# Matmul with batch norm on one core: one more block turned raw, late copies of x by VectorE and ScalarE instead of GpSimd, and one block turned by transfer instead of by TensorE

## The chip, the core and the metric

The kernel runs on one core of a Trainium2 chip. TensorE (PE in the profile, its weight loads PEld), VectorE (DVE), ScalarE (ACT), GpSimd (POOL) and SyncE (SP, which here only issues transfers) each work through a queue of their own, in order, and wait for each other by semaphores. The metric is the device time of one execution in microseconds; less is better.

## The reference

```
y = np.matmul(x, weight)                        # (16, 512, 1024) x (1024, 768), float32
mean = np.mean(y, axis=(0, 1), keepdims=True)   # one mean per output column
var = np.var(y, axis=(0, 1), keepdims=True)
y_norm = (y - mean) / np.sqrt(var + eps)
return (gamma * y_norm + beta).astype(np.float32)
```

The 16 x 512 rows of x are taken as 8192 rows. Each of the 768 columns needs its mean and variance over all 8192 rows before any element of it can be stored. x is 32 MB, the output 24 MB.

## The kernel before, in words

x is loaded in 16 chunks of 512 rows, cast to bf16 on the way (L402, issued by POOL), and turned by DVE (L431, L424) so that the sum dimension k lies on the partitions. The 768 columns are six column tiles of 128 (`nt` 0 to 5). Tiles 0 and 1 (`GA` = 2) are computed with rows on the partitions while x streams in (L506). Tiles 2 to 5 are computed with the columns on the partitions: the weights stand still, a chunk of x moves, and eight matmuls of 128x512 (L571) make one chunk of one tile in one PSUM bank. For chunks 0 to 3 (`EARLY`) this happens while x is still arriving; for chunks 4 to 15 it happens tile after tile once x is complete: tile 2, 3, 4, 5. Tile 3 takes the chunks in the order 12 to 15, 4 to 11, tile 4 in the order 4 to 11, 12 to 15.

After each chunk VectorE takes the statistics from PSUM (L707) and ScalarE keeps y in bf16 in SBUF (L711). When a tile's 16 chunks are done, `finish_tasks` aggregates the statistics (L972, VectorE), takes the root (L986, ScalarE) and makes scale and shift (L989 to L993, VectorE). Then the tile goes out in eight blocks of two chunks (`col_block`). A block has to be normalized and turned, because it lies column by row and the output is row by column. There are three ways:

- *xact*: VectorE (ScalarE for tile 2) normalizes y in place (L1022), SP issues a transfer that turns it (L1214), ScalarE converts it to float32 (L1226), SP stores it (L1196).
- *pe*: VectorE normalizes (L1022), TensorE turns eight 128x128 pieces into a PSUM bank (L1040; the planner puts each between two matmuls of a column unit), ScalarE copies it out of PSUM (L1204), SP stores it (L1196). `MODE` says which blocks of a tile use which way; before, all blocks of tile 4 are *pe*.
- *raw* (`RAW`, `raw_turn`, `raw_spread`, `raw_block`): y is turned by transfer before its statistics are known (L1102, right after the last load of x, because chunks 0 to 3 are ready by then). Once they are known, scale and shift are turned from columns into rows: VectorE prepares them (L1135, L1136), four copies gather them into one row (L1139, 32x64), three copies deal the row to all partitions (L1139, 32x256), and ScalarE puts it into a PSUM bank (L1152). Gather and deal can each go to POOL or to ScalarE. Then VectorE multiplies the turned block from that bank (L1168), POOL adds the shift (L1172), SP stores (L1176). Before, blocks 0 and 1 of tiles 2 and 4 are raw.

The last block of tile 4 is held back and stored in the tail (L1246, L1249). Tile 5 is the tail: after its last matmul come the last statistics, the root (L1302), scale and shift (L1315), and then block by block norm (L1339), turn (L1040), copy (L1352) and store (L1355).

For most chunks x is turned so that pairs of k stand side by side. `part_chunk` copies such a chunk into two plain halves (`x_pl`, L543), four copies of 128x1024 a chunk, so that later matmuls read it without a stride. Chunks 4, 5, 7, 8, 9 and 10 (`PARTED`) are copied early, by ScalarE. Chunks 12 to 15 (`LATE`) are copied after tile 3 has read them, for tiles 4 and 5; the engine is chosen by the planner from those listed.

The order of the work is made by a list planner (`arrange`): every piece of work is a task with a due time, an engine or a choice of engines with a guessed duration, and slots in pools (eight PSUM banks, SBUF tiles, a ring of SBUF words). It places the tasks in a simulated order, and the program then issues them in that order on each engine. All stores and transposing transfers share SP's queue in that order.

The numbering of lines is that of the kernel before; in the changed kernel lines after L1116 stand two to five lines further down.

Of the kernel before, what the change touches and what calls it, by code (L numbers as in the profile page):

```python
# [227 lines left out]
def kernel(  # L228
# [19 lines left out]
    P = 128  # L248
# [14 lines left out]
    EARLY = 4  # L263
# [3 lines left out]
    GY = 2  # L267
# [4 lines left out]
    XT, YB, SQ = C - EARLY, 28, 3  # L272
    ADDED = (0,6,16,28,40)
    PARTED, LATE, SINGLE = (4,5,7,8,9,10), (12,13,14,15), (2,3,6)
    MODE = {2:'xact',3:'xact',4:('pe',)*8}
    MODE = {nt: m if isinstance(m, tuple) else (m,) * (C // GY) for nt, m in MODE.items()}
    RAW, RAWADD, RAWDUE = {2:(0,2),4:(0,2)}, {2:'POOL',3:'POOL',4:'POOL'}, {2:14.0,3:8.0,4:8.0}
    RING = 3 * CH // 32 * KQ // 2
    ENG = {"ACT": nc.scalar, "DVE": nc.vector, "POOL": nc.gpsimd, "SP": nc.sync}

# [39 lines left out]
    sum2 = singles.tile([P, 2 * NA], f32)  # L320
    sum3 = singles.tile([P, 2 * NA], f32)
# [33 lines left out]
    def task(prio, engines, emit, deps=(), lock=False, **kw):  # L355
        t = Task(prio, engines, emit, deps, **kw)
        t.lock = lock
        tasks.append(t)
        return t
# [14 lines left out]
    STORE, XBAR = 1 / 350.0, 1.25  # L374
# [63 lines left out]
    at = M - CH  # L438
# [5 lines left out]
    for kind, n, *n1 in order:  # L444
# [12 lines left out]
        if m0 == M // 2:  # L457
# [6 lines left out]
            dma=(rows * K * 4 / 1024 + 384 * also) * PER_KB * 1.024, takes=[slot])  # L464
# [4 lines left out]
        for i in range(rows // QR):  # L469
            c, q = divmod(m0 // QR + i, QPC)  # L470
# [9 lines left out]
        if rows % QR:  # L480
            t0 = rows // QR * QR // 32
            m1 = m0 + 32 * t0
            c, q = divmod(m1 // QR, QPC)
# [40 lines left out]
    def part_chunk(c, now, engines, small=False, step=0.0, after=()):  # L524

        src = x_slot[c]
        slots = [Slot(sqs if jw < SQ else ys) for jw in range(JW)] if small else [Slot(xts)] * JW
        ts = []

        def copy(jw):  # L530
            def emit(eng):
                if small:
                    if jw < SQ:
                        x_pl = sqpool.tile([P, 2, CH], bf16, tag="sq")
                    else:
                        x_pl = ypool.tile([P, 2, CH], bf16, tag="y")
                    slots[jw].tile = [x_pl]
                elif jw == 0:
                    x_pl = xtpool.tile([P, JW, 2, CH], bf16, tag="xT")
                    slots[0].tile = [x_pl[:, i] for i in range(JW)]  # L540
                dst = slots[jw].tile[0 if small else jw]
                pairs = src.tile[:, jw].rearrange("p m e -> p e m")
                seq(nc.scalar.copy(dst, pairs) if eng == "ACT" else ENG[eng].tensor_copy(dst, pairs))  # L543
            return emit

        for jw in range(JW):
            new = small or jw == 0
            ts.append(task(
                now + step * jw, engines, copy(jw), [x_ready[c, q, JW] for q in range(QPC)] + list(after) + ([] if new else ts[:1]),
                len(engines) > 1, uses=[src] + ([] if new else [slots[jw]]), takes=[slots[jw]] if new else []))  # L550
        plain[c] = slots, ts, small
# [41 lines left out]
    clock = [12.0]  # L593
# [29 lines left out]
    def col_unit(nt, c, jws, q0=0, q1=QPC):  # L623
        slot = bank_of.setdefault((nt, c), None) or Slot(banks)
        bank_of[nt, c] = slot
        first = jws[0] == 0 and q0 == 0
        xs = [plain[c][0][jw] for jw in jws] if c in plain else [x_slot[c]]
        kw = {"takes": [slot], "uses": xs} if first else {"uses": [slot] + xs}
        t = pe_task((1.728 if c in plain or c in SINGLE else 1.808) * len(jws) / JW * (q1 - q0) / QPC,
                    mm(nt, c, list(jws), slot, q0, q1),  # L630
                    waits(jws, c, q0, q1) + ([plain[c][1][jw] for jw in jws] if c in plain else []), (nt, c), **kw)
        if q1 - q0 == QPC:
            t.hosts = 4
        if jws[-1] == JW - 1 and q1 == QPC:
            col_stats(nt, c, slot, t)
        return t
# [60 lines left out]
    col_end = {}  # L697
# [148 lines left out]
    U = clock[0] - 30.0  # L846
# [66 lines left out]
    U = S - 30.0  # L913
# [38 lines left out]
    k = 0  # L952
# [139 lines left out]
    for c in range(RC, C):  # L1092
        ga_block(c, S - 29.8 + 35.5 * (c - RC))

    def raw_turn(nt, c):

        yslot, slot = y_of(nt, c), Slot(ys)

        def xbar(eng):
            r_sb = ypool.tile([P, GY * RT, P], bf16, tag="y")  # L1100
            slot.r = r_sb
            bi = nc.sync.dma_start_transpose(slot.r, y(nt, c, GY))  # L1102
            if not gated:
                tc.add_manual_dep(
                    bi.ins, gate.ins.name,
                    mybir.DependencyInfo(mybir.DependencyClass.Sync, mybir.DependencyReason.DATA),
                    reason="behind the loads",
                )
                gated.append(bi)
            seq(bi)  # L1110

        b = task(U, {"SP": (1.4, 1.4)}, xbar, [col_end[nt, c + i][1] for i in range(GY)] + [gate], dma=XBAR,
                 takes=[slot], uses=[yslot])
        raw[nt, c] = slot, b

    raw, gated, raw_aff = {}, [], {}  # L1116
    gate = last_loads[-1]
    for nt in RAW:
        for c in RAW[nt]:
            raw_turn(nt, c)  # L1120

    def raw_spread(nt, fin_task):
        bank = Slot(banks)
        k = sorted(RAW).index(nt)
        row = sum2[:, 2 * P * k:2 * P * (k + 1)].rearrange("p (i n) -> p i n", n=P)
        wide, turned = sum1[:, NA + 64 * k:NA + 64 * (k + 1)], sum3[:, 64 * k:64 * (k + 1)]
        both = turned.rearrange("p (i n) -> p i n", n=32)
        now = clock[0] + RAWDUE[nt] + 2.0

        def quadrant(i):  # L1130
            return slice(32 * i, 32 * i + 32)

        def turn(eng):
            for i, src in enumerate((scale, shift)):
                seq(nc.vector.tensor_copy(wide[:, quadrant(i)], src[:, nt:nt + 1].to_broadcast([P, 32])))  # L1135
            seq(nc.vector.transpose(turned, wide))  # L1136

        def move(eng, dst, src):
            seq(nc.scalar.copy(dst, src) if eng == "ACT" else nc.gpsimd.tensor_copy(dst, src))  # L1139

        def gather(eng):
            for i in range(4):
                move(eng, row[0:32, :, quadrant(i)], both[quadrant(i)])

        def deal(eng):
            for i in range(1, 4):
                move(eng, row[quadrant(i)], row[0:32])

        def keep(eng):
            a_ps = psum.tile([P, CH], f32, tag="b")  # L1150
            bank.tile = a_ps
            seq(nc.scalar.copy(a_ps[:, 0:2 * P], row.rearrange("p i n -> p (i n)")))  # L1152

        d = task(now, dve(0.35), turn, [fin_task], True)
        g = task(now, {"POOL": (0.8, 0.85), "ACT": (0.9, 1.0)}, gather, [d])
        s = task(now, {"POOL": (1.2, 1.25), "ACT": (1.0, 1.1)}, deal, [g])
        t = task(now, act(0.4), keep, [s], takes=[bank])
        raw_aff[nt] = bank, t, s, row[:, 1]
# [26 lines left out]
    def col_block(nt, c, due, fin_task, held=False):  # L1185
# [12 lines left out]
        a = task(due, act(1.144) if nt == GA else dve(0.45), norm(nt, c, GY), [fin_task] + keeps, nt > GA, uses=[yslot])  # L1198
        if MODE[nt][c // GY] == "pe":
            b, bank = turn_block(due + 0.5, nt, m0, count, [a], [yslot])  # L1200
# [11 lines left out]
        def xbar(eng):  # L1212
# [3 lines left out]
        b = task(due + 0.5, {"SP": (1.4, 1.4)}, xbar, [a], dma=XBAR,  # L1216
                 takes=[t_slot] + ([slot] if MODE[nt][c // GY] == "xact" else []), uses=[yslot])
        if MODE[nt][c // GY] == "xpool":
            def store_x(eng):
# [42 lines left out]
    for nt in range(GA, NT - 1):  # L1262
        if nt == NT - 2:
            for i, c in enumerate(LATE):
                part_chunk(c, clock[0] + 0.0 + 4.0 * i, {"POOL": (1.1, 1.15), "DVE": (0.63, 0.7)},
                           i == 0, 4.0 / 4, [col_end[NT - 3, late[-1]][1]])
        for c in CHUNKS[nt]:
            for jws in halves if nt > GA or c > EARLY + 2 else [[jw] for jw in range(JW)]:
                col_unit(nt, c, jws)
        f = finish_tasks(nt)  # L1270
        start = clock[0] + 3.0
        if nt in RAW:
            raw_spread(nt, f)
        for i in range(C // GY):
            if (nt, GY * i) in raw:
                raw_block(nt, GY * i, start + STEP[nt] * i + RAWDUE[nt])
                continue
            if nt == NT - 2 and C // GY - HELD <= i:
                held.append((nt, GY * i, f))
                continue  # L1280
            col_block(nt, GY * i, start + STEP[nt] * i, f)


    nt = NT - 1
# [45 lines left out]
    for c, r0, rows in ends:  # L1330
        due = E + 2.0 + 0.6 * c
        n = max(rows // CH, 1)
# [13 lines left out]
        b, bank = turn_block(due + 0.6 * (n - 1), nt, m0, count, norms, [y_of(nt, c + i) for i in range(n)])  # L1346
# [56 lines left out]
```

## Time and profile before

| what | value |
|---|---|
| median of three runs | 206.69 us (206.57 to 206.7) |
| the profiled execution, its time | 206.43 us |
| the profiled execution, its span | 204.6 us |
| busy: PE, DVE, ACT, POOL | 188.8, 158.5, 140.3, 129.5 us |
| DMA traffic | 48.48 MB, mean 237 GB/s |
| L1040 turns on PE | 112 |
| L543 late copies | 12 on POOL, 4 on DVE |
| transposing transfers | 14 of L1214, 4 of L1102 |

The profile is of one execution. The span runs from its first to its last instruction; the execution's own time is 1.8 us longer. A group's line gives line, engine, operation, tiles and shapes, the count, busy time and the mean of one in ns, and then the idle time ahead of these instructions with what ended it. The chain is followed back from the last instruction to what released it at each step. Matmuls are pipelined, so the record of one is longer than the distance to the next.

### The profile page before, as it was taken

What the parts mean: (1) busy time and instruction counts of PE and PEld (TensorE: products, weight loads), DVE (VectorE), ACT (ScalarE), POOL (GpSimd) and SP (SyncE); (2) the same over time, 40 slices, a digit from 0 to 9 for tenths busy, and PEclk for the clock granted to TensorE, in tenths of its full rate; (3) what the DMA queues carried; (4) which work ended last, traced back from release to release, by engine and by line L of the source; (5) the groups of instructions that cost most, each with busy time, mean ns of one, the idle gap of its engine ahead of it and who ended that gap; (6) DMA issues with size and microseconds to landing.
All of it is one profiled execution on the core that took longest, in us unless ns stands there. A gap on an engine that the chain in (4) does not pass through costs nothing.

```text
span 204.6 us, 3497 instructions
## 1 busy us (share of the span) xinstructions
PE 188.8 (92%) x1203; PEld 115.1 (56%) x1218; DVE 158.5 (77%) x243; ACT 140.3 (69%) x253; POOL 129.5 (63%) x153
## 2 busy tenths in 40 slices
PE   7979999999999999999999999999999999997900
PEld 3457554656488888777875444444444445554600
DVE  4031879999999999969989998978799879737900
ACT  2001461369979999998979766997555868975950
POOL 7776954877499989996404999389978402530000
PEclk9999999999999999999999999999999999999995
DMA  4999999999999999999594898999999999999998
GB/s 76 155 203 195 194 196 196 196 197 196 190 193 197 197 196 197 196 197 195 100 157 165 313 339 314 265 306 329 305 287 215 325 325 318 307 343 298 311 346 246
DMA packets 97522, 48.48 MB, mean 237 GB/s; under 512 B 23264, under 2 KB 96992, under 8 KB 97504
## 3 DMA queue, kind: packets, MB, share of 16 engines
q0 software_dynamic: 34624, 18.36, 65.0%
q1 hardware_dynamic: 62880, 29.90, 52.8%
q8 instruction: 9, 0.15, 0.3%
q14 instruction: 9, 0.07, 0.1%
HBM read 36.71 MB, written 25.17 MB: 302 GB/s over the span
## 4 chain that ended last, share of the span: by engine, by line
PE 79%; DMA 9%; ACT 3%; POOL 2%; issue 1%; DVE 1%; ACTq 0%; DVEq 0%; POOLq 0%
PE y_ps L571 50%; PE y_ps L506 21%; DMA w_sb<-in_weight_dram 6%; PE y_ps L810 4%; ACT o_sb L1352 3%; DMA ring<-in_x_dram 3%; PE o_ps L1040 2%; POOL ring L402 1%; PE y_ps L749 1%; POOL w_sb L386 1%; DVE xT_sb L431 1%; PE a_ps L899 1%; PE o_ps L1070 0%; ACTq L1398 0%; PE tot_ps L867 0%
## 5 line engine op out<-in xcount | busy, mean ns | idle before, releaser
L571 PEld LDWEIGHTS <-w_sb 128*128 128x128 bf16 x520 | 50.3, 97 | 57.6
L571 PE MATMUL y_ps<-xT_sb,w_sb 128*128 128x512 bf16 (+1 forms) x264 | 58.7, 371 | 0.4
L571 PE MATMUL y_ps<-x_pl,w_sb 128*128 128x512 bf16 x241 | 56.7, 379 | 0.4
L402 POOL DMA_DIRECT2D ring<-in_x_dram x76 | 47.3, 628 | 13.8 <-DVE xT_sb L424 5.0
L506 PE MATMUL y_ps<-w_sb,xT_sb 128*128 128x256 bf16 x448 | 50.5, 273 | 1.8 <-DMA ring<-in_x_dram 1.4
L506 PEld LDWEIGHTS <-xT_sb 128*128 128x128 bf16 x448 | 43.6, 98 | 9.4 <-DVE xT_sb L431 2.7
L431 DVE STREAM_TRANSPOSE xT_sb<-ring 128x1024 f32<-128x1024 f32 (+1 forms) x29 | 31.2, 1111 | 13.6 <-DMA ring<-in_x_dram 13.5
L711 ACT CAST y_sb<-y_ps 128x512 bf16<-128x512 f32 x51 | 29.1, 590 | 15.0 <-DVE stats L707 11.3
L707 DVE BATCH_NORM_STATS2 stats<-y_ps 128x6 f32<-128x512 f32 x46 | 30.8, 686 | 10.1 <-PE y_ps L571 9.8
L938 POOL TENSOR_TENSOR ring<-ring,sum 128x1024 f32<-128x1024 f32 (+1 forms) x11 | 23.7, 2182 | 15.0 <-DVE ring L933 14.9
L655 ACT ACTIVATE sq_sb<-y_ps 128x512 f32<-128x512 f32 x28 | 16.5, 613 | 17.1 <-PE y_ps L506 16.4
L662 POOL TENSOR_TENSOR sum<-sum,sq_sb 128x512 f32<-128x512 f32 x20 | 25.6, 1278 | 3.5 <-ACT sq_sb L655 2.3
L543 ACT COPY x_pl<-xT_sb 128x1024 bf16<-128x1024 bf16 x24 | 24.4, 1054 | 1.7 <-DVE xT_sb L431 1.7
L658 DVE TENSOR_TENSOR sum<-y_ps,sum 128x512 f32<-128x512 f32 x28 | 18.9, 675 | 6.4 <-ACT sq_sb L655 5.4
L668 ACT CAST y_sb<-y_ps 128x512 bf16<-128x512 f32 x28 | 16.0, 602 | 7.6 <-DVE sum L658 7.4
L933 DVE TENSOR_TENSOR ring<-y_sb,a_ps 128x1024 f32<-128x1024 bf16 (+1 forms) x16 | 16.7, 1077 | 0.1
L1040 PE MATMUL o_ps<-ident,y_sb 128*128 128x128 bf16 x112 | 14.8, 220 | 1.6 <-DVE y_sb L1339 1.5
L1226 ACT CAST ring<-ring 128x1024 f32<-128x1024 bf16 x14 | 14.7, 1049 | 1.8 <-DMA ring<-y_sb 1.8
L543 POOL COPY x_pl<-xT_sb 128x1024 bf16<-128x1024 bf16 x12 | 13.3, 1139 | 2.1 <-DVE x_pl L543 2.0
L424 DVE STREAM_TRANSPOSE xT_sb<-ring 128x2048 bf16<-128x2048 bf16 x6 | 13.5, 2288 | 0.2 <-DMA ring<-in_x_dram 0.2
L1139 POOL COPY sum<-sum 32x256 f32<-32x256 f32 (+1 forms) x10 | 3.4, 344 | 12.4 <-ACT sum L1139 11.6
L587 PE MATMUL idle_ps<-idle_sb 128*128 128x512 f32 x18 | 9.6, 685 | 1.5 <-DVE idle_sb L315 1.5
(105 smaller groups left out, 163.4 us busy)
## 6 DMA issues: line engine op xcount, KB each, us to landing
out_dram<-ring SPq DMA_DIRECT2D x37, 512.0 KB, 3.7
ring<-in_x_dram POOLq DMA_DIRECT2D x52, 256.0 KB, 8.7
out_dram<-o_sb SPq DMA_DIRECT2D x6, 512.0 KB, 4.8
ring<-in_x_dram POOLq DMA_DIRECT2D x16, 128.0 KB, 6.1
w_sb<-in_weight_dram POOLq DMA_DIRECT2D x8, 192.0 KB, 6.1
out_dram<-ring SPq DMA_DIRECT2D x6, 256.0 KB, 3.0
ring<-in_x_dram POOLq DMA_DIRECT2D x4, 192.0 KB, 7.8
out_dram<-o_sb SPq DMA_DIRECT2D x3, 256.0 KB, 2.6
```

The source lines that it names most:

```text
L402: bi = seq(nc.gpsimd.dma_start(x_bf[32 * i:32 * i + 32], src[:, :, KQ * i:KQ * (i + 1)]))
L431: seq(nc.vector.transpose(dst, src[:, :, jw0:jw1]))
L506: seq(nc.tensor.matmul(y_ps[:, s], x_of(c, jw, e, t * P, (t + 1) * P), w_sb[:, jw, e, 0:NA], start=(s == 0 and jw == 0 and e == 0), stop=( ...
L543: seq(nc.scalar.copy(dst, pairs) if eng == "ACT" else ENG[eng].tensor_copy(dst, pairs))
L571: seq(nc.tensor.matmul(y_ps, w_sb[:, jw, e, nt * P:(nt + 1) * P], moving(c, jw, e, q0 * QR, q1 * QR, parted), start=(jw == 0 and e == 0 an ...
L658: seq(nc.vector.tensor_add(sum1, slot.tile[:, 0:n], sum1))
L662: seq(ENG[eng].tensor_add(acc, acc, state["sq"][:, 0:n]))
L707: seq(nc.vector.bn_stats(dst, slot.tile))
L711: seq(nc.scalar.copy(y(nt, c), slot.tile))
L933: seq(nc.vector.tensor_mul(slot.o, y_row[c].y[:, s0:s1], aff[0][:, None, :].to_broadcast([P, n, NA])))
L938: seq(ENG[eng].tensor_add(slot.o, slot.o, row[:, None, :].to_broadcast([P, n, NA])))
L1040: seq(nc.tensor.transpose(dst, src, ident))
```

## The change

Three things are changed together.

1. `RAW` gets block 0 of tile 3. Its transfer is issued with the four other early ones, and tile 3 gets a spread of its own (a third row of scale and shift, placed in `sum3`), one VectorE multiply, one POOL add and one store, in place of norm, transfer, convert and store.
2. Block 2 of tile 4 (chunks 4 and 5) goes the way *xact* instead of *pe*.
3. The late copies of chunks 12 to 15 are offered to VectorE and ScalarE instead of POOL and VectorE.

`raw_turn` also takes a due time and could turn later blocks; no block of this change uses that.

```diff
-    MODE = {2:'xact',3:'xact',4:('pe',)*8}
+    MODE = {2:'xact',3:'xact',4:('pe',)*2+('xact',)*1+('pe',)*5}
     MODE = {nt: m if isinstance(m, tuple) else (m,) * (C // GY) for nt, m in MODE.items()}
-    RAW, RAWADD, RAWDUE = {2:(0,2),4:(0,2)}, {2:'POOL',3:'POOL',4:'POOL'}, {2:14.0,3:8.0,4:8.0}
+    RAW, RAWADD, RAWDUE = {2:(0,2),3:(0,),4:(0,2)}, {2:'POOL',3:'POOL',4:'POOL'}, {2:14.0,3:8.0,4:8.0}
...
-    def raw_turn(nt, c):
+    def raw_turn(nt, c, due):
...
-        b = task(U, {"SP": (1.4, 1.4)}, xbar, [col_end[nt, c + i][1] for i in range(GY)] + [gate], dma=XBAR,
+        b = task(due, {"SP": (1.4, 1.4)}, xbar, [col_end[nt, c + i][1] for i in range(GY)] + [gate], dma=XBAR,
                  takes=[slot], uses=[yslot])
...
     for nt in RAW:
         for c in RAW[nt]:
-            raw_turn(nt, c)
+            if c < EARLY:
+                raw_turn(nt, c, U)
...
         k = sorted(RAW).index(nt)
-        row = sum2[:, 2 * P * k:2 * P * (k + 1)].rearrange("p (i n) -> p i n", n=P)
+        acc, at = ((sum2, 0), (sum2, 2 * P), (sum3, 2 * P))[k]
+        row = acc[:, at:at + 2 * P].rearrange("p (i n) -> p i n", n=P)
...
             for i, c in enumerate(LATE):
-                part_chunk(c, clock[0] + 0.0 + 4.0 * i, {"POOL": (1.1, 1.15), "DVE": (0.63, 0.7)},
+                part_chunk(c, clock[0] + 0.0 + 4.0 * i, {"DVE": (0.63, 0.7), "ACT": (1.05, 1.1)},
                            i == 0, 4.0 / 4, [col_end[NT - 3, late[-1]][1]])
...
+        for c in RAW.get(nt, ()):
+            if c >= EARLY:
+                raw_turn(nt, c, clock[0])
```

In the order in which the changed program's instructions then stand, seven late copies are on ScalarE and nine on VectorE; POOL's queue after the adds of tiles 0 and 1 holds only the spreads and the raw adds; the gather of tile 4's spread is on POOL and its deal on ScalarE (before: the other way round); TensorE's turns of tile 4 stand beside chunks 7 to 10 of tile 5 (before: 8 to 12); and chunk 15 of tile 4 is computed in one piece (before: in two halves, between halves of chunks 4 and 5 of tile 5).

## The prediction

> **What bounds the kernel now.** I read the page's busy shares and chain first, then the chain in order of time, then a table by stage, then the groups by line, last the engines' timelines.
>
> ```profile
> PE 188.8 (92%) x1203; PEld 115.1 (56%) x1218; DVE 158.5 (77%) x243; ACT 140.3 (69%) x253; POOL 129.5 (63%) x153
> ...
> PE 79%; DMA 9%; ACT 3%; POOL 2%; issue 1%; DVE 1%; ACTq 0%; DVEq 0%; POOLq 0%
> ```
>
> TensorE carries 79% of the chain. In order of time (start, length, what) the chain stays on PE from 25.95 to 187.29 us:
>
> ```profile
> 171.06 0.06 PE o_ps L1040
> 171.12 0.22 PE y_ps L571
> 171.33 0.06 PE o_ps L1040
> ...
> 187.05 0.24 PE o_ps L1040 x4
> ...
> 187.94 0.20 ACT std L1302
> ...
> 190.04 4.74 ACT o_sb L1352 x6
> ```
>
> The reader is to see two things: a turn on PE (L1040) takes 0.06 us out of the chain between two matmuls, and after PE's last column unit comes a tail: root, norms, copies and stores of tile 5. By stage (length; PE, PEld, DVE, ACT, POOL busy; clock; DMA share; GB/s):
>
> ```profile
> 143.00:150.00 7.00, 6.95 (x33) 3.21 (x33) 5.50 (x10) 3.15 (x6) 6.94 (x7) 1.00 1.14 313
> 150.00:158.00 8.00, 7.94 (x38) 3.56 (x37) 8.00 (x13) 5.66 (x8) 5.99 (x6) 1.00 1.12 228
> 158.00:170.40 12.40, 12.35 (x58) 5.59 (x58) 9.79 (x20) 9.12 (x13) 2.98 (x3) 1.00 1.20 325
> ...
> 178.00:188.20 10.20, 9.45 (x67) 5.55 (x66) 5.11 (x13) 7.00 (x13) 2.84 (x2) 1.00 1.14 342
> 188.20:189.30 1.10, 0.27 (x3) 0.13 (x4) 1.03 (x5) 0.68 (x2) 0.00 (x0) 1.00 0.50 149
> 189.30:191.50 2.20, 2.16 (x27) 1.45 (x26) 2.20 (x8) 2.11 (x5) 0.00 (x0) 1.00 0.96 289
> ```
>
> PE is full wherever the change acts, at full granted clock. VectorE is full in 150-158; ScalarE has room; the stores have spare time in 150-158 and at 188-191. So only what shortens PE's own work, or makes PE wait, moves the end.
>
> **The change part by part.** Groups by line (busy, mean ns of one; idle before):
>
> ```profile
> L543 ACT COPY x_pl<-xT_sb 128x1024 bf16<-128x1024 bf16 x24 | 24.4, 1054 | 1.7 <-DVE xT_sb L431 1.7
> L1040 PE MATMUL o_ps<-ident,y_sb 128*128 128x128 bf16 x112 | 14.8, 220 | 1.6 <-DVE y_sb L1339 1.5
> L1226 ACT CAST ring<-ring 128x1024 f32<-128x1024 bf16 x14 | 14.7, 1049 | 1.8 <-DMA ring<-y_sb 1.8
> L543 POOL COPY x_pl<-xT_sb 128x1024 bf16<-128x1024 bf16 x12 | 13.3, 1139 | 2.1 <-DVE x_pl L543 2.0
> L1172 POOL TENSOR_TENSOR ring<-ring,sum 128x1024 f32<-128x1024 f32 x4 | 9.5, 2387 | 2.1 <-issue 2.1
> L543 DVE COPY x_pl<-xT_sb 128x1024 bf16<-128x1024 bf16 x4 | 3.1, 796 | 0.0
> ```
>
> *Block 2 of tile 4 by transfer.* Eight L1040 turns leave PE. While turns are interleaved the matmul starts go 171.22, 171.50, 171.77: 0.2717 us a pair, against 0.2159 us for a plain matmul (32 in 6.91 us from 134.26). So one turn is 0.056 us and eight are **0.45 us off the path**. The turns stop one chunk earlier; the other blocks' turns are the same. ScalarE reads the transfer's result (1049 ns) instead of PSUM (1015 ns, L1204): the same work. One DMA transpose is added at about 169-170.
>
> Here a rule speaks for far more. The row says 220 ns for one turn but they start 0.056 us after the matmul before. The Trainium skill, "TensorE: Matmul & The Clock Gate", Part 4, puts a turn in one kernel's context at about 275 ns; an estimate by that is 8 x 0.275 = 2.2 us. By the trace's starts it is 0.45 us, and the sum goes by these.
>
> *Block 0 of tile 3 raw.* Its transpose moves from about 150 to the head of SP's queue, behind the four others (6.34 us for four, 1.6 each, ending at 106.2). SP then waits 2.9 us for L1060 before the first store at 109.08, so 1.6 us hides there. Tile 3 loses one y norm (655 ns) and one L1226 on ScalarE, and gains L1135/L1136 (0.6-0.8 us) and one L1168 (1214 ns) on DVE, 2.2 us of gather and deal plus one L1172 (2387 ns) on POOL, and one L1152 (388 ns) on ACT that holds a PSUM bank for some 4 us. All off PE. In tile 4's own spread the gather goes to POOL and the deal to ACT: three 32x256 copies there, which the trace does not show. Bounds: 243 ns (ACT, 32x64) and 421 ns (POOL, 32x256); nearest 388 ns (ACT, 128x256), so 1.2 us.
>
> *Late copies.* POOL loses 12 copies (13.3 us). In the built order ACT gets 7 (7 x 1.054 = 7.4 us), DVE 5 more (9 in all; 5 x 0.796 = 4.0 us). ACT idles 3.85 us in 143-150, 2.34 in 150-158, 1.0 in 140-143: 7.2 us against 7.4 + 0.4 - 1.0 = 6.7. Just enough. DVE has only 1.7 us in 140-158 against 4.0 + 0.8 + 0.6 = 5.4, but gets some back: beside POOL's copies its small operations are slow.
>
> ```profile
> 147.87 0.87 DVE L992 TENSOR_TENSOR scale<-rstd,gamma_sb 128x1 f32<-128x1 f32 x1
> 148.66 1.05 DVE L993 SCALAR_TENSOR_TENSOR shift<-tmp,rstd,beta_sb 128x1 f32<-128x1 f32 x1
> ...
> 168.60 0.16 DVE L992 TENSOR_TENSOR scale<-rstd,gamma_sb 128x1 f32<-128x1 f32 x1
> 168.68 0.21 DVE L993 SCALAR_TENSOR_TENSOR shift<-tmp,rstd,beta_sb 128x1 f32<-128x1 f32 x1
> ```
>
> The same two cost 1.92 us beside POOL and 0.37 us without; with L989 (0.52 against 0.14) that returns 1.9 us. So DVE is some 2 us behind PE at 158 and has 12.40 - 9.79 = 2.6 us of idle in 158-170 to recover. Cover: eight PSUM banks, about 14 us of PE at 1.73 us a chunk, against a bank's turn-round of 4-5 us. Walking ACT and DVE through their new queues with these rows, the last late copy ends near 158; chunk 15 reads it at 162. The change also adds a wait: DVE's L1168 of block (3,0) needs ring space that ACT's third L1226 of tile 3 frees, near 158.2; behind it stand the statistics of chunks 11 to 14 of tile 4, in step again by 162.3. Cost to PE: nothing. Without that cover every us behind would be a us of PE.
>
> *What is next in line.* Two places are tight.
> First, the earlier turns. Block 3 is now turned beside chunk 7 of tile 5, not block 2 beside chunk 8. In before, chunk 12 of tile 4 starts at 156.87 and chunk 6 of tile 5 at 167.23: six chunks of 1.727 us. Chunk 15 now runs unbroken and ends at 163.8, so: statistics 164.0-164.7, L972 to 165.3, root 165.6, L989-L993 to 166.15, held block's norm to 166.7, statistics of chunk 4 to 167.3; those of chunk 5 wait for PE (167.43) and end at 168.1; two L1022 (pair 1.0 us) end at 169.05. PE reaches the turn's weight load at 167.23 + 1.73 = 168.96: 0.1 us early, and the chain has 0.2 us of idle ahead of chunk 5's statistics. I take 0; bounds 0 and 0.1 us if the walk holds.
> Second, the turn beside chunk 10 needs the bank that ACT's keep of chunk 7 frees. ACT: gather done 171.3, deals to 172.4, two L1226, L1152 and the keep to 175.0; PE is there at 175.7. 0.65 us to spare: 0.
>
> *Transfers.* SP waits for block (3,0)'s add (about 162) and for the norm of block (4,2) (168.6), so stores bunch: ten follow the last transpose from 170.3, as before (170.48). My walk has a hole near 173, then nine at 1.51 us (512 KB at 347 GB/s) until 187.8; before, the queue drained at 188.2. Cost nothing: the tail's spare transfer time is 1.10 x (1 - 149/347) + 2.20 x (1 - 289/347) = 1.0 us.
>
> *Sum.* The profiled execution took 206.43 us, span 204.6, 1.8 around it; 206.43 - 0.45 = 205.98. The three runs' median is 0.26 above the profiled one: 206.69 - 0.45 = **206.24 us**.
>
> **The rivals.**
> *A turn costs its whole record.* PE would gain 8 x 0.220 = 1.76 us: 204.93. For it: the 220 ns. Against: the starts above. The page named there would end at 206.69 - 2.2 = 204.49 by its figure. Chance 5%.
> *The stores set the end.* The added transpose costs the transfers 0.95 us late in the run (a transpose and a store take 2.45 us in 158-170, a store 1.51). If all of it stands before the tail it uses up the 1.0 us of spare: 206.69 - 1.0 + 0.95 = 206.64, no change. For it: 342 GB/s in 178-188. Against: as many stores follow the last transpose as before, and the last turned block's copy is ready about 1 us sooner (walk: 181.9 against 182.8). The Trainium skill, "DMA: Bandwidth & Descriptors", Where 436 GB/s comes from, has HBM bind stores at about 358 GB/s; the trace agrees with 342 in the last 11 us. Chance 10%.
> *VectorE is late at the first turned block.* Slower. Place: chunk 7 of tile 5. ACT's root (L986) now stands right behind an L1226 that waits for a transpose, in the fullest stretch of ACT and DVE. Once the root is more than 0.3 us later than 165.6, PE waits us for us; a whole L1226 in the way makes 1.05 - 0.3 = 0.75 us, and if the chain is already at its limit 1.05: 206.69 - 0.45 + 1.05 = 207.29. For it: ACT's 6.7 us of new work in 7.2 of idle, DVE's 2 us of lag. Against: that transpose should have landed 2 us before ACT reaches its L1226. Chance 23%.
>
> **How the numbers follow.** Forecast 62%, rivals 5, 10 and 23%. About 0.2% (0.41 us) is what a measurement of this kernel can tell from no change. The forecast lies just beyond it; with the 0.1 us wait it is within, for which I take 6 of its 62 points. Faster: 56 + 5 = 61%. Same: 6 + 10 = 16%. Slower: 23%. Range: 205.8 (the forecast with the tail's 1.0 us of spare partly won back, some 0.4) to 207.3 (the whole L1226); it leaves out the 5% and the worst of the 23%. The forecast's own: 206.1 to 206.4.
>
> **What would show it.** Right: 104 L1040 matmuls for 112; PE unbroken to about 186.6 and the root L1302 near 187.5; L543 7 on ACT, 9 on DVE, none on POOL; L992/L993 of tile 3 short; no PE wait at 168-170 or at 175-176. Wrong: PEld L1040 waiting for DVE's L1022, PE waiting for ACT's copies, or a queue of stores still moving at 189.

## The result and the profile after

The changed kernel is slower. Over 22 runs of each the median went from 206.56 to 207.0 us; the ratio is 1.0028, with a 95% interval from 1.0018 to 1.0037, so some 0.58 us more by the ratio (0.44 by the medians). The forecast was 206.24 us and faster. The profiled execution of the changed kernel took 207.0 us with a span of 205.2; that of the kernel before 206.43 with 204.6. The two spans differ by 0.61 us, and the two traces show all of it.

TensorE did what the forecast said. The page of the changed kernel, busy times and shares of the chain by engine:

```profile
PE 190.8 (93%) x1210; PEld 115.1 (56%) x1210; DVE 159.3 (78%) x251; ACT 145.6 (71%) x259; POOL 121.4 (59%) x150
...
PE 79%; DMA 9%; ACT 3%; POOL 2%; DVE 1%; issue 1%; ACTq 0%; DVEq 0%; POOLq 0%
```

The chain of the changed kernel in order of time (start, length, what):

```profile
186.67 0.24 PE o_ps L1040 x4
...
187.56 0.20 ACT std L1307
...
189.65 4.74 ACT o_sb L1357 x6
```

Before, these three stood at 187.05, 187.94 and 190.04. Everything that TensorE paces, the copies of tile 5 to `o_sb` too, begins 0.38 to 0.39 us earlier than before. The root is L1302 in the kernel before and L1307 here; below I take its start by the engine's own record, 187.84 and 187.46.

Groups of the changed kernel by line and shape (busy us, mean ns of one; idle before):

```profile
L543 ACT COPY x_pl<-xT_sb 128x1024 bf16<-128x1024 bf16 x31 | 31.7, 1061 | 1.7 <-DVE xT_sb L431 1.7
L1228 ACT CAST ring<-ring 128x1024 f32<-128x1024 bf16 x14 | 14.8, 1058 | 2.3 <-DMA ring<-y_sb 2.3
L1040 PE MATMUL o_ps<-ident,y_sb 128*128 128x128 bf16 x104 | 13.1, 221 | 1.6 <-DVE y_sb L1344 1.5
L1174 POOL TENSOR_TENSOR ring<-ring,sum 128x1024 f32<-128x1024 f32 x5 | 12.2, 2454 | 10.6 <-DVE ring L1170 6.5 <-issue 4.0
L543 DVE COPY x_pl<-xT_sb 128x1024 bf16<-128x1024 bf16 x9 | 5.8, 678 | 0.0
```

The turns are 104, the late copies 7 on ScalarE and 9 on VectorE, GpSimd has none and adds five raw blocks. What TensorE waited for (total us, times, longest):

```profile
PE o_ps L1040 <- DVE y_sb L1344: 1.5, 1, 1.5
PE idle_ps L587 <- DVE idle_sb L315: 1.5, 1, 1.5
PE y_ps L506 <- DVE xT_sb L431: 0.2, 1, 0.2
```

None of these lies at one of the two tight places; the first is the tail's own norm, which was in the profile before as well.

So the loss lies after TensorE's work, in the transfers. By stretch (length; PE, PEld, DVE, ACT, POOL busy; granted clock; DMA share; GB/s), first the kernel before:

```profile
188.00:188.80 0.80, 0.00 (x0) 0.00 (x0) 0.56 (x4) 0.80 (x3) 0.00 (x0) 1.00 0.34 99
188.80:189.60 0.80, 0.54 (x4) 0.23 (x4) 0.80 (x4) 0.34 (x2) 0.00 (x0) 1.00 0.96 293
202.70:203.10 0.40, 0.00 (x0) 0.00 (x0) 0.00 (x0) 0.00 (x0) 0.00 (x0) 0.50 1.13 341
203.10:203.50 0.40, 0.00 (x0) 0.00 (x0) 0.00 (x0) 0.00 (x0) 0.00 (x0) 0.50 0.12 32
```

and the same stretches of the changed kernel:

```profile
188.00:188.80 0.80, 0.16 (x2) 0.11 (x2) 0.76 (x4) 0.50 (x2) 0.00 (x0) 1.00 1.16 348
188.80:189.60 0.80, 0.76 (x9) 0.40 (x8) 0.80 (x4) 0.64 (x2) 0.00 (x0) 1.00 1.13 341
202.70:203.10 0.40, 0.00 (x0) 0.00 (x0) 0.00 (x0) 0.00 (x0) 0.00 (x0) 0.50 0.20 54
203.10:203.50 0.40, 0.00 (x0) 0.00 (x0) 0.00 (x0) 0.00 (x0) 0.00 (x0) 0.50 0.07 22
```

The reader is to see two things. Before, the transfers rested at 188.0 (99 GB/s over 0.8 us), ahead of the last stores; after, they do not (348). And the bulk of the stores ends earlier after (54 GB/s at 202.7 where before had 341), but then 22 GB/s go on to 203.5. The packet records say what these 22 GB/s are: single packets of 512 bytes, one every 0.0235 us, which is 21.8 GB/s or one sixteenth of 348. I read them as one of the 16 DMA engines that still has work when the others are done (two of them for the first 0.2 us). I call it the trickle, and measure it from the last moment at which more than half of the usual 18 packets are under way: 0.21 us before, 0.78 us after. The last packet lands at 203.36 before and 203.53 after.

From there to the end of the span it took 1.25 us before and 1.69 us after. SP's closing waits show why (total us, times, longest), first the kernel before, then the changed one:

```profile
SPq L1398 <- DMA out_dram<-o_sb: 2.7, 3, 1.5
```

```profile
SPq L1403 <- DMA out_dram<-o_sb: 3.6, 1, 3.6
```

Three waits became one long one. At the end SP asks for the semaphores of its transfers in a fixed order, one instruction after another. These are SP's records of that (time at which each was passed, semaphore):

```
before  200.656 S108  200.718 S110  200.782 S112  200.844 S113  200.903 S115  201.444 S116  202.944 S117  203.703 S118
after   203.888 S108  203.950 S110  204.014 S112  204.076 S113  204.135 S115  204.196 S116  204.256 S117  204.317 S118
```

SP's transfers take these eight semaphores in turn. Before, SP issues 88, and the last store holds S118, the last one asked for. The change adds one transfer, the last store moves to S108, which is asked for first, and the seven other questions, 0.06 us each, come only after it: 0.43 us.

The account of the profiled span, each term the difference of two numbers above: root -0.38; root to last packet 15.52 before and 16.07 after, +0.55; last packet to end +0.44. Sum +0.61 of 0.61.

### The profile page after: what moved, and what is told of

Read it like the earlier page. It is cut to its first block, busy times and chain, and to the rows that moved or that the text cites. A ratio compares the mean times of both kernels' runs of the same rounds, so it can differ in the third digit from the quotient of the medians.

```text
span 205.2 us, 3510 instructions
## 1 busy us (share of the span) xinstructions
PE 190.8 (93%) x1210; PEld 115.1 (56%) x1210; DVE 159.3 (78%) x251; ACT 145.6 (71%) x259; POOL 121.4 (59%) x150
## 4 chain that ended last, share of the span: by engine, by line
PE 79%; DMA 9%; ACT 3%; POOL 2%; DVE 1%; issue 1%; ACTq 0%; DVEq 0%; POOLq 0%
PE y_ps L571 50%; PE y_ps L506 21%; DMA w_sb<-in_weight_dram 6%; PE y_ps L810 4%; ACT o_sb L1357 3%; DMA ring<-in_x_dram 3%; PE o_ps L1040 1%; POOL ring L402 1%; PE y_ps L749 1%; POOL w_sb L386 1%; DVE xT_sb L431 1%; PE a_ps L899 1%; PE o_ps L1070 0%; ACTq L1403 0%; PE tot_ps L867 0%
## 5 line engine op out<-in xcount | busy, mean ns | idle before, releaser
L571 PE MATMUL y_ps<-xT_sb,w_sb 128*128 128x512 bf16 (+1 forms) x272 | 59.3, 371 | 0.0
L571 PE MATMUL y_ps<-x_pl,w_sb 128*128 128x512 bf16 x248 | 57.4, 379 | 0.0
L543 ACT COPY x_pl<-xT_sb 128x1024 bf16<-128x1024 bf16 x31 | 31.7, 1061 | 1.7 <-DVE xT_sb L431 1.7
L1174 POOL TENSOR_TENSOR ring<-ring,sum 128x1024 f32<-128x1024 f32 x5 | 12.2, 2454 | 10.6 <-DVE ring L1170 6.5
L1040 PE MATMUL o_ps<-ident,y_sb 128*128 128x128 bf16 x104 | 13.1, 221 | 1.6 <-DVE y_sb L1344 1.5
L1141 POOL COPY sum<-sum 32x64 f32<-32x64 f32 (+1 forms) x18 | 5.6, 309 | 13.7 <-DVE sum L1138 13.0
L587 PE MATMUL idle_ps<-idle_sb 128*128 128x512 f32 x18 | 11.2, 782 | 1.5 <-DVE idle_sb L315 1.5
```

The source lines that it names most:

```text
L571: seq(nc.tensor.matmul(y_ps, w_sb[:, jw, e, nt * P:(nt + 1) * P], moving(c, jw, e, q0 * QR, q1 * QR, parted), start=(jw == 0 and e == 0 an ...
```

## The experiments

Theory A: the order of the closing waits costs about 0.4 us, and it depends on nothing but the number of SP's transfers. Theory B: the trickle comes from a DMA engine that falls behind while the stores stream without a rest, and the change takes away the rest in which it catches up. (In the expectations of the first four runs B still has a looser form, that the stores end later because of the added transpose; B2, in the later ones, is B with the stream counted from 175 us.) Against B stood D, that the trickle is made in the tail itself by the `o_sb` stores, and C, that the raw block and the late copies are what delayed the stores.

### Theory A: moving the last store from semaphore to semaphore

One, three, seven or eight tiny loads are issued on SP some 55 us into the kernel, right behind the loads of gamma and beta, which changes only the count. On the kernel before and on the changed one:

```diff
+        for _ in range(N):
+            seq(nc.sync.dma_start(touched[0:32, 0:2], first_rows[0, :, 0:2, 0:TOUCH]))
```

**b_plus1**, the kernel before, N = 1.

> The kernel before with one more tiny transfer (256 bytes) on SP's queue, right after the loads of gamma and beta at about 46 us, where SP then waits 45 us for the last load. Nothing else is changed. It shifts by one which of the eight transfer semaphores the last store signals: the first of SP's eight closing waits instead of the last. Theory A (in the changed kernel the last store signals the semaphore that SP's closing waits ask for first, so seven more waits of 0.06 us follow its landing): 0.35 to 0.45 us slower than before, TensorE's end unchanged. Theory B (the stores of the tail simply end later, because of the added transpose): no change, within 0.1 us.

**b_plus8**, the kernel before, N = 8.

> The same with eight tiny transfers: the last store signals the same semaphore as before. Theory A: no change, within 0.1 us, which shows that tiny transfers at this place cost nothing themselves. Theory B: no change. Were it slower by eight times what one costs, the price would lie in the tiny transfers.

**a_plus7**, the changed kernel, N = 7.

> The changed kernel with seven tiny transfers at the same place: the last store then signals the semaphore that the closing waits ask for last, as in the kernel before. Theory A: 0.35 to 0.45 us faster than the changed kernel, so 0.0 to 0.1 us around the kernel before (TensorE ends 0.4 us sooner, the last transfers do not). If the closing waits were all that went wrong: 0.4 us faster than before. Theory B: like the changed kernel, 0.45 us slower than before.

**a_plus3**, the changed kernel, N = 3.

> The changed kernel with three tiny transfers: the last store signals the fourth semaphore of the eight, so four waits follow its landing instead of seven. Theory A: between the changed kernel and the one with seven, 0.18 us faster than the changed kernel, about 0.2 to 0.3 us slower than before. Theory B: like the changed kernel.

Measured, 12 runs of each beside 35 of the kernel before (206.37):

| run | median us | ratio, 95% interval | last packet to end |
|---|---|---|---|
| b_plus1, last store on the semaphore asked for first | 206.76 | 1.0019 [1.0007, 1.0031] | 1.68 |
| b_plus8, on the one asked for last | 206.38 | 1.0000 [0.9988, 1.0012] | 1.27 |
| a_plus3, in the middle | 206.73 | 1.0016 [1.0000, 1.0032] | 1.50 |
| a_plus7, on the one asked for last | 206.54 | 1.0003 [0.9990, 1.0016] | 1.26 |

One load that does nothing costs the kernel before 0.39 us, eight of them nothing. The wait of b_plus1 has the changed kernel's form, one in place of three:

```profile
SPq L1400 <- DMA out_dram<-o_sb: 3.1, 1, 3.1
```

Theory A holds. It is worth 0.41 to 0.44 us, and with it taken out the changed kernel is level with the one before. That is still not the gain of 0.38 us that TensorE hands over; theory B is about that.

### The parts of the change

**mode_plus7**, the transfer of the tile 4 block alone, N = 7 as above:

```diff
-    MODE = {2:'xact',3:'xact',4:('pe',)*8}
+    MODE = {2:'xact',3:'xact',4:('pe',)*2+('xact',)*1+('pe',)*5}
```

> The kernel before with one part of the change, the second block of tile 4 turned by a transfer, and seven tiny loads at the start, so that the last store again holds the semaphore that SP asks for last; copies of x and the raw blocks as before. Theory B (the pause of the transfers near 188 us is what lets a late DMA engine catch up; the transfer takes the pause away): TensorE ends about 0.4 us earlier, there is no stretch under 100 GB/s between 187.5 and 189.5, the bulk of the tail's stores ends 0.3 to 0.4 us earlier, but a trickle of single 512-byte packets goes on to about 203.4 or later; time 206.4 to 206.6, within 0.1% of before. Rival C (what was lost beside the semaphores belongs to the raw block and to the copies of x, whose stores left later): the pause stays at 0.2 us or more, the last packet is near 203.0, and the time is 0.3 to 0.4 us under before, near 206.0.

**raw_late**, the other two parts (88 transfers on SP, none added):

```diff
-    RAW, RAWADD, RAWDUE = {2:(0,2),4:(0,2)}, {2:'POOL',3:'POOL',4:'POOL'}, {2:14.0,3:8.0,4:8.0}
+    RAW, RAWADD, RAWDUE = {2:(0,2),3:(0,),4:(0,2)}, {2:'POOL',3:'POOL',4:'POOL'}, {2:14.0,3:8.0,4:8.0}
...
-                part_chunk(c, clock[0] + 0.0 + 4.0 * i, {"POOL": (1.1, 1.15), "DVE": (0.63, 0.7)},
+                part_chunk(c, clock[0] + 0.0 + 4.0 * i, {"DVE": (0.63, 0.7), "ACT": (1.05, 1.1)},
```

> The kernel before with the other two parts of the change: the first block of tile 3 turned raw and the late copies of x by VectorE and ScalarE, without the transfer for tile 4. As many transfers on SP as before. What the prediction costed at nothing would be nothing: TensorE's last turn near 187.05 as before, the pause near 188 us as before, ratio 0.999 to 1.001. Theory B says the same, as the turns stay on TensorE and no transfer is added. Rival C: later stores leave a shorter pause (under 0.4 us below 100 GB/s) and the time rises by 0.2 to 0.4 us, ratio 1.001 to 1.002.

**late_only**, the late copies alone (the second of these two edits).

> The kernel before with the late copies of x on VectorE and ScalarE alone. As costed in the prediction, nothing: TensorE's last turn near 187.05, ratio 0.999 to 1.001. Theory B2 leaves it there too, and says that the gain in rest of the run with raw block and late copies comes from the raw block: the rest near 188 us stays 0.6 to 1.0 us. If the copies are what cleared GpSimd for earlier stores, the rest is 1.2 us or more.

mode_plus7 took 207.31 us against 206.33, ratio 1.0047 [1.0032, 1.0062]: clearly slower, where theory B had expected no change; B had the lost rest and the trickle right, and their size wrong. raw_late took 206.22, ratio 0.9998 [0.9984, 1.0012]; late_only 206.68 against 206.52, 1.0007 [0.9991, 1.0022], no difference that can be told. The tables by stretch, mode_plus7 first, then raw_late:

```profile
188.00:189.00 1.00, 0.66 (x6) 0.35 (x7) 1.00 (x4) 0.53 (x3) 0.00 (x0) 1.00 1.15 347
...
203.00:203.80 0.80, 0.00 (x0) 0.00 (x0) 0.00 (x0) 0.00 (x0) 0.00 (x0) 0.50 0.08 25
```

```profile
187.20:188.00 0.80, 0.08 (x2) 0.00 (x0) 0.56 (x4) 0.80 (x3) 0.00 (x0) 1.00 0.09 27
188.00:188.80 0.80, 0.00 (x0) 0.00 (x0) 0.73 (x4) 0.66 (x2) 0.00 (x0) 1.00 0.16 51
...
203.10:203.50 0.40, 0.00 (x0) 0.00 (x0) 0.00 (x0) 0.00 (x0) 0.00 (x0) 0.50 0.00 0
```

With the transfer alone there is no rest at all, and the trickle is 1.47 us long, to 203.97. With the two other parts the rest is longer than before, and late engines can be seen working alone in it (27 GB/s at 187.2 to 188.0: two engines to 187.4, at 42 GB/s, then one, at 21); nothing is left of them at the end. So C falls: the raw block and the late copies bring the stores forward, and it is the transfer that takes the rest away. SP's queue shows where. In the kernel before and in the changed one, the first two stretches from the last transfers to the stores behind them (start, length, count):

```profile
168.66 1.73 SPq L1214 DMA_TRANSPOSE ring<-y_sb  x1
170.48 7.15 SPq L1196 DMA_DIRECT2D out_dram<-ring  x5
```

```profile
167.00 4.55 SPq L1216 DMA_TRANSPOSE ring<-y_sb  x3
171.65 6.44 SPq L1198 DMA_DIRECT2D out_dram<-ring  x5
```

Ten whole-block stores follow the last transfer in both, but they begin 1.17 us later after the change. In raw_late they begin at 169.80, in mode_plus7 at 173.30.

### Theory B: giving the rest back

**a7_less** and **b_less**: the changed kernel with N = 7, and the kernel before, with most of one store of tile 3 left out. In the kernel before the block goes through `col_block`, whose store is cut in the same way.

```diff
+            w = 1 if (nt, c) == (3, 0) else n
...
-                out_flat[m0:m0 + n * P, nt * P:(nt + 1) * P].rearrange("(s p) n -> p s n", p=P), slot.o))
+                out_flat[m0:m0 + w * P, nt * P:(nt + 1) * P].rearrange("(s p) n -> p s n", p=P), slot.o[:, 0:w]))
```

> The changed kernel with seven tiny loads, and of the store of the first block of tile 3 only an eighth is written (64 KB in place of 512 KB; seven eighths of that block's output are left out). The 448 KB are 1.3 us of transfers at the 348 GB/s of this stretch. Theory B: the pause near 188 us comes back, about 1 us long, the late engine catches up in it, no trickle over 0.25 us is left at the end, and the run gains what TensorE had gained: 0.3 to 0.4 us under the same kernel with the whole store, ratio to before 0.998 to 0.9985 (206.0 to 206.1). Rival D (the trickle is made in the tail itself, by the o_sb stores, whatever went before): pause or not, the last packet stays near 203.4 and the time within 0.1 us of the kernel with the whole store, ratio 1.000 to 1.0005.

> The kernel before with the same store cut to an eighth (448 KB not written, so seven eighths of that block's output are left out), the control of the one above. Theory B: the transfers already pause near 188 us and the late engine already catches up, so a longer pause (about 1.9 us) gives only the 0.1 us of trickle that is left: ratio 0.9993 to 1.000. If the tail as a whole hung on the amount of transfers, it would gain up to 1.3 us: ratio 0.994.

a7_less took 206.97 us, ratio 1.0028 [1.0011, 1.0044]; b_less 206.45, 1.0005 [0.9987, 1.0024]. Both expectations missed in the same way: the rest near 188 us did not change (none, and 0.70 us as before). The 448 KB were taken out ahead of a stretch at 172 to 176 us in which the transfers are not full anyway, as SP's stores wait there for ScalarE's copies; that hole grew (172 to 174 us: 173 GB/s in b_less, 307 in the kernel before), and the stream behind it stayed what it was. The stream that counts begins at about 175 us. A trickle of 1.05 us without a rest, in a7_less, and of 0.07 us with one, in b_less, fits B but does not test it. That a7_less is no faster than a_plus7 (1.0003), with fewer bytes to store, also fits.

**a7_cut4** and **b_cut4**: the same cut, on a store inside that stream.

```diff
+            if (nt, c) == (4, 8):
+                seq(ENG[eng].dma_start(dst()[:, 0:1], slot.o[:, 0:1]))
+                return
             seq(ENG[eng].dma_start(dst(), slot.o))
```

> The changed kernel with seven tiny loads (last store on the semaphore asked for last), and of one store of tile 4, that of the chunks 8 and 9, only an eighth is written (448 KB of output left out). That store lies in the stretch from 176 to 188 us in which the transfers never rest. Theory B2 (a DMA engine falls behind, by about 1 us, while the stores of ring stream without a rest from 175 us on; only a rest lets it catch up, and the kernel before had one of 0.8 us at 188): a rest of about 1 us comes back before the o_sb stores, the trickle at the end shrinks from 0.85 us to under 0.3 us, the last packet lands near 202.9 in place of 203.5, and the run takes 0.4 to 0.6 us less than the same kernel with the whole store, ratio to before 0.9975 to 0.9985. Rival D (the trickle belongs to the o_sb stores): rest or not, the trickle stays over 0.6 us and the ratio is 1.000 to 1.001.

> The kernel before with the same store of tile 4 cut to an eighth (448 KB of output left out). Theory B2: the rest near 188 us grows from 0.8 to about 2 us, but the engine had caught up in it already, but for a trickle of 0.1 to 0.2 us: ratio 0.9990 to 1.0000. If the whole amount of the transfers set the end, it would be 0.994.

a7_cut4 took 206.08 us against 206.52, ratio 0.9973 [0.9957, 0.9989]; b_cut4 206.53, 0.9999 [0.9985, 1.0013]. The same bytes left out are worth 0.62 us to the changed kernel (a_plus7 at 1.0003, a7_cut4 at 0.9973, each by its ratio to the kernel before that ran beside it; by their intervals 0.2 to 1.0 us) and nothing that can be told to the kernel before. By stretch, a7_cut4 and then b_cut4:

```profile
187.20:188.00 0.80, 0.21 (x4) 0.03 (x1) 0.64 (x3) 0.73 (x3) 0.00 (x0) 1.00 0.56 167
188.00:188.80 0.80, 0.00 (x0) 0.00 (x0) 0.65 (x4) 0.79 (x3) 0.00 (x0) 1.00 0.16 47
...
203.10:203.50 0.40, 0.00 (x0) 0.00 (x0) 0.00 (x0) 0.00 (x0) 0.00 (x0) 0.50 0.00 0
```

```profile
187.20:188.00 0.80, 0.62 (x10) 0.43 (x7) 0.56 (x2) 0.47 (x2) 0.00 (x0) 1.00 0.12 37
188.00:188.80 0.80, 0.00 (x0) 0.00 (x0) 0.56 (x4) 0.80 (x3) 0.00 (x0) 1.00 0.07 20
```

The rest is back in a7_cut4 (1.15 us), and the trickle falls from 0.74 to 0.08 us. D falls, B holds. And what is left between these two, with the closing waits alike and the rest in both, is TensorE's share at last: root at 187.75 against 188.16, 0.41 us earlier; medians 206.08 and 206.53, 0.45 us; ratios 0.9973 and 0.9999, 0.54 us.

### Is there a place for the transfer that keeps the gain?

**raw2_plus7**, the changed kernel, N = 7, `RAW` of tile 3 (0,2) in place of (0,).

> A version that might beat both: the changed kernel with seven tiny loads and with the second block of tile 3 turned raw too. In the run with the raw block and the late copies alone the stores of ring were done at 186.7 in place of 188.1, so a raw block of tile 3 is worth about 1.3 us of rest; a second one would bring a rest back in front of the o_sb stores. Theory B2: TensorE still ends 0.4 us before that of the kernel before, the rest is 0.5 to 1.2 us, the trickle under 0.4 us, ratio 0.998 to 0.9995. If VectorE or GpSimd is late with the added block (5.3 us of work on GpSimd), TensorE waits for a bank or the stores come as late as now: ratio 1.000 to 1.003.

**mode3_plus7** and **mode5_plus7**, the changed kernel, N = 7, with the transfer on the fourth and the sixth block of tile 4.

> The changed kernel with seven tiny loads and the transfer put on the fourth block of tile 4 in place of the third. If the transfer's own time takes the rest away, there is still none near 188 us, the trickle is 0.6 us or more and the ratio 1.000 to 1.003; if its place did it, a rest of 0.4 us or more is back, the trickle is under 0.4 us and the ratio 0.998 to 0.9995.

> The same with the transfer on the sixth block of tile 4. As for the fourth block: no rest, a trickle of 0.6 us or more and 1.000 to 1.004 if the transfer's own time is what counts; a rest of 0.4 us or more and 0.998 to 0.9995 if its place does. A transfer this late could also bring its block's store later than the o_sb stores, which would cost 0.5 us or more, ratio over 1.003.

**raw_mode_plus7**, the changed kernel, N = 7, with the late copies on GpSimd and VectorE as before.

> The changed kernel with seven tiny loads and the late copies of x on GpSimd and VectorE again, as before the change. If the copies have no part in it: no rest, a trickle of 0.6 to 0.9 us, ratio 1.000 to 1.0015, as with them. If GpSimd's copies delay the raw blocks' sums (2.35 us each), and these the stores, the trickle is over 1 us and the ratio over 1.002.

**raw_late_2**, raw_late once more.

> The raw block and the late copies without the transfer, once more. In its first run the o_sb stores began 0.2 us earlier and the ratio was 0.9998 with an interval of 0.0014 to either side. If the profiled 0.2 us are real, 0.9985 to 0.9995; if not, 0.9995 to 1.0005. Theory B2 gives nothing beyond the 0.1 us of trickle.

| run | median us | ratio, 95% interval |
|---|---|---|
| raw2_plus7 | 207.9 (before 206.52) | 1.0062 [1.0043, 1.0082] |
| mode3_plus7 | 206.9 (before 206.39) | 1.0017 [1.0004, 1.0030] |
| mode5_plus7 | 206.94 | 1.0021 [1.0007, 1.0034] |
| raw_mode_plus7 | 208.59 | 1.0100 [1.0079, 1.0120] |
| raw_late_2 | 206.33 | 0.9995 [0.9982, 1.0007] |

raw2_plus7 and raw_mode_plus7 ran six times, the others twelve. None beats the kernel before by an amount that can be told; raw_late_2 lies on the border of its two expectations and does not decide between them. The hope for a second raw block was wrong: the stores behind the last transfer begin at 174.86 there, later and not sooner, with ScalarE's conversions and GpSimd's sums ahead of them in SP's waits. On two other blocks the transfer takes the rest away just as well, so its own time counts more than its place. The late copies, which alone change nothing, are needed once the transfer and the raw block are there (the transfer with the late copies but without the raw block was not run). GpSimd's sums of tile 4's two raw blocks, in the changed kernel and in raw_mode_plus7:

```profile
175.63 4.72 POOL L1174 TENSOR_TENSOR ring<-ring,sum 128x1024 f32<-128x1024 f32 x2 [4.00 <-issue]
```

```profile
178.58 4.88 POOL L1176 TENSOR_TENSOR ring<-ring,sum 128x1024 f32<-128x1024 f32 x2 [2.20 <-DVE ring L1172]
```

The sums come 2.95 us later, SP's last ring store of a whole block at 186.27 in place of 184.30, and the `o_sb` stores queue behind.

### All runs in one table

The profiled execution of each; us; rest is the idle share of the DMA engines between 186 and 189.4 us, added up.

| run | root | root to last packet | rest | trickle | last packet to end |
|---|---|---|---|---|---|
| before | 187.84 | 15.52 | 0.70 | 0.21 | 1.25 |
| b_plus1 | 187.82 | 15.45 | 0.70 | 0.17 | 1.68 |
| b_plus8 | 187.84 | 15.38 | 0.69 | 0.07 | 1.27 |
| late_only | 188.53 | 15.43 | 1.04 | 0.11 | 1.27 |
| raw_late | 187.62 | 15.38 | 1.84 | 0.10 | 1.27 |
| raw_late_2 | 187.68 | 15.39 | 1.82 | 0.10 | 1.26 |
| b_less | 187.93 | 15.39 | 0.70 | 0.07 | 1.27 |
| b_cut4 | 188.16 | 15.39 | 1.97 | 0.10 | 1.26 |
| a7_cut4 | 187.75 | 15.38 | 1.15 | 0.08 | 1.26 |
| after | 187.46 | 16.07 | 0.01 | 0.78 | 1.69 |
| a_plus3 | 187.28 | 16.03 | 0.01 | 0.71 | 1.50 |
| a_plus7 | 187.43 | 16.06 | 0.01 | 0.74 | 1.26 |
| a7_less | 187.11 | 16.34 | 0.01 | 1.05 | 1.25 |
| mode3_plus7 | 188.03 | 16.10 | 0.01 | 0.78 | 1.26 |
| mode5_plus7 | 187.79 | 16.64 | 0.01 | 1.28 | 1.25 |
| mode_plus7 | 187.12 | 16.85 | 0.01 | 1.47 | 1.25 |
| raw2_plus7 | 187.38 | 17.56 | 0.01 | 1.74 | 1.27 |
| raw_mode_plus7 | 187.26 | 18.39 | 0.01 | 1.45 | 1.26 |

With a rest of 0.69 us or more, the time from root to last packet is 15.4 to 15.5 us in every kernel; without one it is 16.0 or more. In most of these the whole difference is the trickle; in the last two the bulk of the stores is late as well. The root itself moves by a few tenths from one profiled execution to another for reasons outside this study (late_only, mode3_plus7), which is why the columns count from it.

When an engine falls behind can be read from the traces. Each transfer of SP raises its semaphore 16 times, and I take each time as one DMA engine's. How long after the middle of its 16 times a store gets the last one then says how far the last engine is behind. In us:

| store | before | a7_cut4 | after | mode_plus7 |
|---|---|---|---|---|
| last one that landed ahead of the load below | 0.09 | 0.90 | 0.76 | 0.09 |
| first one that landed behind that load | 1.60 | 1.30 | 1.37 | 1.48 |
| last whole block, ahead of the rest | 1.57 | 1.25 | 1.32 | 1.44 |
| first of the held block's two, behind the rest | 0.77 | 0.35 | 1.32 | 1.49 |
| fourth `o_sb` store | 0.21 | 0.12 | 0.80 | 1.45 |
| last `o_sb` store | 0.21 | 0.08 | 0.78 | 1.46 |

So the engine does not fall behind little by little, and theory B has to be put more narrowly: it is put back in one step and keeps that distance as long as the stores stream. The step falls on a load of 16 KB of the program's own instructions, at 179.09 us before and at 179.56 us after. The transfers' views of 178 to 182 us show it as one packet, first the kernel before, then the changed one:

```profile
q8 instruction: 1, 0.02, 2.0%
```

```profile
q8 instruction: 1, 0.02, 1.5%
```

All 18 traces have this load, between 179 and 182 us, and the last engine is 1.3 to 1.9 us behind right after it in each. Loads of 8 KB do the same to a second engine where they fall into the stream (0.76 us in the changed kernel, from the one at 175.10 us). The kernel before has the arrears just as the changed one has; what differs is the rest. Three gaps among the first `o_sb` stores, 0.43 us together, give the changed kernel 0.5 us back; mode_plus7 has none of them and keeps all.

What stays open: no run moves or removes such a load, so its part is read from time and size alone; and which engine it is, as the records give no engine numbers.

## Why the prediction was wrong

- *Block 2 of tile 4 by transfer, 0.45 us off the path.* Right in kind, a little large: the root moved by 0.38 us, between the cut kernels by 0.41, so 0.05 us a turn. The rival of a whole record (1.76 us) fell. The Trainium skill, "TensorE: Matmul & The Clock Gate", Part 4, puts a turn in one kernel's context at about 275 ns; as a price on TensorE's path this trace does not bear it out, and the measured 0.05 us decides.
- *Block 0 of tile 3 raw, and the late copies, at nothing.* Right: raw_late 0.9998 and 0.9995, late_only 1.0007. The copies stood 7 and 9, L992 and L993 of tile 3 took 0.16 and 0.21 us for 0.87 and 1.05. One size was off: the walk had the raw block's sum done near 162; VectorE's multiply waited 1.15 us for ring space and the store left at 163.87.
- *The two tight places.* Right: no wait of TensorE at either, so the rival of a late VectorE (207.29, 23%) came near the measured time by a mechanism that did not occur.
- *Transfers, cost nothing.* This is the step that failed, in two ways. It counted one more transpose as time on the DMA engines against 1.0 us of spare, and had the stores behind the last transpose begin at 170.3; they began at 171.65, and the walk's end at 187.8 became a queue that never drained, the last of the signs named under wrong. And it took the idle time in the tail for something that nobody used. It was used: one DMA engine, 1.57 us behind ahead of the rest and 0.77 us right behind it in the kernel before, worked off its arrears there. Without the rest that engine ends the kernel 0.55 us later in relation to the root.
- *The sum*, 206.43 - 0.45, let all that follows TensorE move with it as it stood. It lacked a term that has nothing to do with load: SP's 89th transfer turns the semaphores by one, and the closing waits cost 0.44 us more (b_plus1: 0.39 us without any other change). The prediction had the extra DMA in its hand and priced it as bytes and as issue time, but not as a count.
- *The rival that the stores set the end* (206.64, 10%) had the right part of the kernel, but only as the loss of the gain. The 342 GB/s that it leaned on need no common limit: an engine that works alone moves 21.8 GB/s, a sixteenth of the full stream's 348. With the closing waits on top the time went beyond before. That 207.0 lies inside the stated range, 205.8 to 207.3, is luck: its upper end came from the late VectorE.

The Trainium skill, "DMA: Bandwidth & Descriptors", Why a DMA increments its semaphore by 16 and not by 1, says that only the full count over the engines means that a transfer's data have landed. The trace agrees: SP passes the last store's semaphore at 203.888, 0.36 us after the trickle's last packet at 203.53, though the bulk of the stores had ended at 202.75.

## What to carry to other kernels

At the end of a kernel the last transfer to land is not the whole tail: count the transfers on the issuing queue, see which semaphore the last store gets and where it stands in the closing waits, and let it be the one asked for last; here a dummy load is worth or costs 0.4 us. Idle time of the DMA engines ahead of the last stores is not spare as long as one engine is behind the others: look at what trickles on in it, and for loads of instructions in the stream before it, before spending it. A gain on the engine that bounds the kernel arrives only if the transfers behind it were waiting for that engine, and it can be tested by cutting the bytes of one store in the stream ahead.

## What the runs showed of the hardware that was not expected

- A tiny load on SP, 55 us into the kernel, makes it 0.39 us slower, seven more make it as fast as without (206.76, 206.38, 206.37 us). Each closing question costs 0.06 us once its semaphore is there.
- In a stream of 512 KB stores at 346 GB/s, one of the 16 DMA engines was 1.3 to 1.9 us behind the others right after a load of 16 KB of instructions, in all 18 traces. It kept that distance while the stores streamed (1.48 us at 181.7 us and 1.46 at the end in mode_plus7) and worked its arrears off, at 21.8 GB/s, only while the others rested.
- Leaving 448 KB out of one store was worth 0.62 us at one place of the changed kernel and nothing at another some 15 us earlier, as the transfers waited for data in between.
